# A PEER transformer's V stage: its own loading step for gates and results, four places per ring, and gathered rows handed out in other numbers

## The chip, the cores and the metric

The kernel runs on one core of a Trainium2 chip. The metric is the device time in microseconds of one execution. The kernel before took 2890.41 us (median of three runs, 2883.72 to 2892.33).

## The reference

Two layers, each with a mixer and a PEER feed-forward, over 256 latent and 256 context tokens of width 1024. The feed-forward picks 16 of 16,384 experts in each of 8 heads for every token and sums their V rows, weighted by a gate times the GELU of the product with their U rows:

```python
best_s, best_j = lax.top_k(cand_s.reshape(PEER_CHUNK, PEER_HEADS, PEER_TOPK * PEER_TOPK), PEER_TOPK)
idx = jnp.take_along_axis(cand_i.reshape(PEER_CHUNK, PEER_HEADS, PEER_TOPK * PEER_TOPK), best_j, axis=-1)
g = jax.nn.softmax(best_s, axis=-1)
a = jnp.einsum('td,thkd->thk', t, u[idx])
w = (jax.nn.gelu(a.astype(jnp.float32)) * g).astype(t.dtype)
return jnp.einsum('thk,thkd->td', w, v[idx])
```

Layer 0 has the even mixer (neighbourhood attention and a Fourier mix), layer 1 the odd mixer (differential attention). The feed-forward runs on latent and context tokens in layer 0 and on latent tokens alone in layer 1; a last norm closes the kernel.

## The kernel before

The feed-forward is done densely for most tokens. A U stage multiplies all tokens of a layer by all 16,384 rows of U; a V stage multiplies the result, weighted with gates that are zero for experts not chosen, by all rows of V. Each float32 operand is split into a high and a low part, and three products are summed.

The **U stage** (`u_prep`, `u_mm`) runs over 32 chunks of 512 experts, four loads `du` of 512 KB each, and 48 matmuls (L670 to L672) per chunk. The GELU of the result stays in SBUF for the last chunks (`dy`; 8 chunks of layer 0 and 11 of layer 1, `KEEP`) and goes to DRAM (`ad`) for the others.

The **V stage** runs over 64 chunks of 256 experts, first those whose result is resident (16 in layer 0, 22 in layer 1), then those that were written out (48 and 42). `load_v` issues on SP the loads of a chunk: the gates `dg` (384 KB in layer 0, 256 KB in layer 1), for a written-out chunk its result `dyl` (256 KB), and two halves of V, `dv`, of 512 KB each; all three rings have three places. `v_prep` makes the high part `dvh` on ACT (L724) and the low part `dvl` on DVE (L725), which frees the place in the ring `dv`. `w_prep` multiplies result and gates on DVE (L746), transposes the product on PE (L733) and splits it (`dwh`, `dwl`, and `dxh`, `dxl` for the second context tile). `v_mm` does 36 matmuls per chunk in layer 0 and 24 in layer 1, beside 6 and 4 transposes. The V pool of layer 0 takes 63 KB per partition and that of layer 1 56 KB; both lie in SBUF beside the pool of the U stage, without overlap.

The **first context tile** of layer 0 does not take part in the dense stages. Its rows are gathered, one expert per token at a time: POOL gathers `row` (512 KB, ring of four places, L549), DVE adds it up (L564 for U; `gacc`, L576, for V). A generator `rows` gives 128 rows of U for the second context tile (a gate table follows), 128 of U and 128 of V for the first. `feed(n)` asks it for n steps: 5 per U chunk for 26 chunks, 2 for the six after, 3 per V chunk, 6 in each of the eight steps of the odd mixer.

A scheduler sets the order of instructions on each engine from the program's order and from what each may start on; an engine works its own list in order. So loads of the V stage can stand among those of the U stage on SP, and rows asked for in the mixer can stand before the end of the V stage. At the end of V in layer 0, DVE adds the sums to x (`yadd` L583, L584), POOL works out the reciprocal root (L255 to L258) from `rstd` (L253), DVE normalises (`xn`, L332), and PE transposes for the odd mixer (L337).

Of the kernel before, what the change touches and what calls it, by code (L numbers as in the profile page):

```python
# [8 lines left out]
F32 = mybir.dt.float32  # L9
# [8 lines left out]
P = 128  # L18
D = 1024
# [8 lines left out]
NC = 64  # L28
# [121 lines left out]
class Builder:  # L150
# [481 lines left out]
    def dense(self, l, tables, hs, ups, yp, keep, mid, late, fin, ad, beside):  # L632

        nc, V, S, G, T = self.nc, self.V, self.S, self.G, self.T
        U = self.A[f"peer_uT{l}"]  # L640
        Vt = self.A[f"peer_v{l}"].rearrange("(c j) d -> c j d", j=P)
        nt = tables.shape[0]
        away = 2 * (NC // 2 - keep)
        cs = list(range(away, NC)) + list(range(away))
        ut, vs, ldv, gts, ys = {}, {}, {}, {}, {}
        up = ups.enter_context(self.pool("uphase", side="right"))

        def u_prep(c):
            if c >= NC // 2:
                return  # L650
            h, l_ = ut.setdefault(c, ([], []))
            for q in range(4):
                t = up.tile([P, 2, UN], F32, name="du", bufs=3)
                nc.sync.dma_start(t, U[c, :, q * 2:(q + 1) * 2])
                th = up.tile([P, 2, UN], F32R, name="duh", bufs=5)
                tl = up.tile([P, 2, UN], F32R, name="dul", bufs=5)
                S.activation(th, t, AF.Copy)  # L657
                with self.tc.high_priority():
                    V.tensor_tensor(tl, t, th.bitcast(F32), ALU.subtract)  # L659
                h += [th[:, 0, :], th[:, 1, :]]  # L660
                l_ += [tl[:, 0, :], tl[:, 1, :]]

        def u_mm(c):

            uh, ul = ut.pop(c)
            w = self.wide() if c % 2 else None
            bs = [w[:, i * 512:(i + 1) * 512] if c % 2 else self.bank("x") for i in range(2)]
            for k in range(KT):
                for (hi, lo), b in zip(hs, bs):
                    T.matmul(b, lhsT=hi[:, k, :], rhs=uh[k], start=k == 0, stop=False)  # L670
                    T.matmul(b, lhsT=hi[:, k, :], rhs=ul[k], start=False, stop=False)  # L671
                    T.matmul(b, lhsT=lo[:, k, :], rhs=uh[k], start=False, stop=k == KT - 1)  # L672
            if 2 * c < away:
                y = up.tile([P, 2, UN], F32, name="da", bufs=2)
            else:
                y = yp.tile([P, 2, UN], F32, name="dy", bufs=keep)
            if c % 2:
                S.activation(y.rearrange("p i n -> p (i n)"), w, AF.Gelu_apprx_tanh)
            else:
                for i in range(2):  # L680
                    S.activation(y[:, i, :], bs[i], AF.Gelu_apprx_tanh)
            if 2 * c < away:
                nc.sync.dma_start(ad[:, :, c * UN:(c + 1) * UN].rearrange("i p n -> p i n"), y)
            else:
                for hf in range(2):
                    ys[2 * c + hf] = y[:, :, hf * 256:(hf + 1) * 256]

        u_prep(0)
        mid()
        for c in range(NC // 2):  # L690
            u_mm(c)
            u_prep(c + 1)
            beside(c)
        ups.close()
        with self.pool("vphase") as vp:
            w = self.wide()
            pacc = [w[:, 0:512], w[:, 512:1024], self.bank("y"), self.bank("y")]
            if nt == 3:
                pacc = [self.bank("x"), self.bank("x")] + pacc[2:] + pacc[:2]

            def load_v(n):
                if n >= NC:
                    return
                c = cs[n]
                gt = vp.tile([P, nt, 256], F32, name="dg", bufs=3)
                nc.sync.dma_start(gt, tables[:, :, c * 256:(c + 1) * 256].rearrange("i p n -> p i n"))
                gts[n] = gt
                if c < away:
                    ys[c] = vp.tile([P, 2, 256], F32, name="dyl", bufs=3)
                    nc.sync.dma_start(ys[c], ad[:, :, c * 256:(c + 1) * 256].rearrange("i p n -> p i n"))  # L710
                ldv[n] = []
                for a in range(2):
                    t = vp.tile([P, D], F32, name="dv", bufs=3)
                    nc.sync.dma_start(t, Vt[2 * c + a])
                    ldv[n].append(t)

            def v_prep(n):
                if n >= NC:
                    return
                vh, vl = [], []  # L720
                for v in ldv.pop(n):
                    th = vp.tile([P, D], F32R, name="dvh", bufs=3)
                    tl = vp.tile([P, D], F32R, name="dvl", bufs=3)
                    S.activation(th, v, AF.Copy)  # L724
                    V.tensor_tensor(tl, v, th.bitcast(F32), ALU.subtract)  # L725
                    vh.append(th)
                    vl.append(tl)
                vs[n] = vh, vl

            def w_split(name, src, m):  # L730
                b = self.bank("c", m * P)
                for a in range(m):
                    T.transpose(b[:, a * P:(a + 1) * P], src(a), self.ident)  # L733
                wh = vp.tile([P, m, P], F32R, name=name + "h", bufs=2)
                wl = vp.tile([P, m, P], F32R, name=name + "l", bufs=2)
                b2 = b.rearrange("p (a t) -> p a t", a=m)
                S.activation(wh, b2, AF.Copy)
                V.tensor_tensor(wl, b2, wh.bitcast(F32), ALU.subtract)
                return wh, wl

            def w_prep(c):
                if c >= NC:
                    return
                y = ys.pop(cs[c])
                g = gts.pop(c)
                V.tensor_tensor(y, y, g[:, 0:2, :], ALU.mult)  # L746
                ws[c] = [w_split("dw", lambda a: y[:, a // 2, a % 2 * P:a % 2 * P + P], 4)]
                if nt == 3:
                    ws[c].append(w_split("dx", lambda a: g[:, 2, a * P:(a + 1) * P], 2))

            def mm(b, w, a, v, first, last):
                wh, wl = w[0][:, a, :], w[1][:, a, :]
                T.matmul(b, lhsT=wh, rhs=v[0], start=first, stop=False)  # L753
                T.matmul(b, lhsT=wh, rhs=v[1], start=False, stop=False)  # L754
                T.matmul(b, lhsT=wl, rhs=v[0], start=False, stop=last)  # L755

            def v_mm(c):
                vh, vl = vs.pop(c)
                w = ws.pop(c)

                for a, i, hf in [(a, i, hf) for a in range(2) for i in range(nt) for hf in range(2)]:
                    hs = slice(hf * 512, (hf + 1) * 512)
                    mm(pacc[2 * i + hf], w[i // 2], 2 * (i % 2) + a, (vh[a][:, hs], vl[a][:, hs]),
                       c == 0 and a == 0, c == NC - 1 and a == 1)

            ws = {}
            load_v(0)
            v_prep(0)
            load_v(1)
            w_prep(0)  # L770
            for c in range(NC):
                v_prep(c + 1)
                load_v(c + 2)
                w_prep(c + 1)
                v_mm(c)
                next(late, None)
                beside(NC // 2 + c)
            for _ in late:
                pass
            fin(pacc, vp)  # L780

    def ffn(self, l, modT, h, wp, wclose, keep, nt=2, late=iter(()), finish=None, beside=lambda c: None):
# [4 lines left out]
        with self.pool("ypool") as yp:  # L787
# [15 lines left out]

            def fin(pacc, vp):

                self.tmp = Slots((yp, "dy", keep), (vp, "dv", 3))
                g = self.gate(modT, 5, 1, "c", self.tmp, None, None)
                y = self.tmp.tile([P, D], F32, name="yadd")
                for i in range(2):
                    self.add_ffn(2 + i, pacc[2 * i:2 * i + 2], g, y)  # L810
                if finish is not None:
                    finish(pacc[4:])
# [3 lines left out]
    def run(self):  # L816
# [118 lines left out]
        def feed(n):  # L935
            for _ in range(n):
                next(rows, None)

        def beside(c):

            with tc.issue_after(routed) if c < 1 else ExitStack():
                feed(5 if c < 26 else 2 if c < NC // 2 else 3)

        def finish(pacc):
            self.norm_T(1, sc1, "x", *hl)
# [23 lines left out]
    def odd_mixer(self, cp, mp, wk, wp, sc, modT, hl, rows, feed):  # L969
# [65 lines left out]
        for c in range(4):  # L1035
            self.project_T(qT[:, c * 2:c * 2 + 2, :], self.weight2(wp, w_in[c]), hl, "x", scale=0.125)
            for m in range(2):
                rotate(qT[:, c * 2 + m, :])
            feed(6)
        for c in range(4):  # L1040
            self.project_T(kTs[1][:, c * 2:c * 2 + 2, :], self.weight2(wp, w_in[4 + c]), hl, "x")
            for m in range(2):
# [1 line left out]
            self.project(vs[1][:, :, c * 256:(c + 1) * 256], self.weight2(wp, w_in[8 + c]), hl, "x")  # L1044
            if 3 + c < 5:
                self.modulation(1, 3 + c, modT, wk, "y", 4)
            feed(6)
        feed(4 * P)

        hc = [Halves(*(rows.tile([P, KT // 2, 256], F32R, name=f"oh{c}{i}", tag="row", bufs=ROWBUFS) for i in range(2)))  # L1050
# [43 lines left out]
```

## Time and profile before

| | us |
|---|---|
| median of three runs | 2890.41 |
| the profiled execution | 2891.71 |
| its span in the trace | 2889.9 |
| layer 0, last matmul of U to last of V | 1096.7 to 1665.2 |
| layer 0, end of V to first transposes of the odd mixer | 1665.2 to 1689.1 |
| layer 1, last matmul of U to end of V | 2437.9 to about 2865 |

Over the span PE is busy for 2610.9 us (90%), DVE for 2038.6 (71%), ACT for 1310.6 (45%) and POOL for 562.0 (19%). The profile gives times in microseconds from the start of the span. SPq is the queue in which SP issues DMAs; the time of a DMA runs from its issue to its landing.

### The profile page before, as it was taken

How to read it: one execution, taken by the hardware profiler on the slowest of the kernel's cores; microseconds unless marked ns; L12 is line 12 of the kernel's file. 1: busy time of each engine (PE TensorE's matmuls, PEld its weight loads, DVE VectorE, ACT ScalarE, POOL GpSimd, SP SyncE). 2: the span in 40 equal slices, each digit the busy share in tenths (PEclk: the TensorE clock that was granted, in tenths of full speed). 3: DMA queues.
4: the chain of work that ended last, by engine and by line, in shares of the span. 5: the costliest groups of instructions: out<-in, count | busy, mean ns of one | idle time of the engine just before them, and what ended most of it. 6: DMA issues, size and time to landing. Idle time of an engine off the chain costs nothing.

```text
span 2889.9 us, 40187 instructions
## 1 busy us (share of the span) xinstructions
PE 2610.9 (90%) x14161; PEld 2134.2 (74%) x14161; DVE 2038.6 (71%) x3904; ACT 1310.6 (45%) x2226; POOL 562.0 (19%) x531
## 2 busy tenths in 40 slices
PE   6999984689999989999999969988999999998786
PEld 4776954567777767888888867868888887886665
DVE  3335699999988877887787874766998555554454
ACT  3334432358673433333333334544599743443332
POOL 0000003343433444433344430000000000000000
PEclk9999997899999999999999979999999999999999
DMA  6453466899999999999999856233778975566664
GB/s 246 132 204 86 160 243 206 278 353 345 354 374 354 358 360 351 351 351 351 338 340 358 316 184 231 91 107 127 238 223 266 313 251 180 180 205 214 201 220 140
DMA packets 354634, 735.49 MB, mean 255 GB/s; under 512 B 35312, under 2 KB 182016, under 8 KB 351872
## 3 DMA queue, kind: packets, MB, share of 16 engines
q1 hardware_dynamic: 299136, 531.56, 54.9%
q0 software_dynamic: 55296, 201.35, 19.5%
q8 instruction: 112, 1.84, 0.3%
q14 instruction: 90, 0.74, 0.1%
HBM read 664.13 MB, written 68.68 MB: 254 GB/s over the span
## 4 chain that ended last, share of the span: by engine, by line
PE 50%; issue 16%; DMA 15%; DVE 9%; POOL 6%; ACT 3%; SPq 1%; DVEq 0%; POOLq 0%; ACTq 0%
DMA dyl<-ad 7%; POOL row L549 5%; PE bank L754 4%; PE bank L755 4%; PE bank L207 4%; PE bank L206 4%; PE bank L753 4%; PE bank L208 4%; DMA du<-in_peer_uT 2%; PE bank L671 2%; PE bank L672 2%; PE wide L755 2%; PE wide L754 2%; PE wide L753 2%; PE bank L670 2%
## 5 line engine op out<-in xcount | busy, mean ns | idle before, releaser
L549 POOL DMA_INDIRECT row<-in_peer_u,gidx x256 | 346.7, 1354 | 530.2 <-DVE row L564 423.8
L724 ACT ACTIVATE dvh<-dv 128x1024 fp32r<-128x1024 f32 x256 | 269.4, 1059 | 393.6 <-DMA dv<-in_peer_v 193.6
L657 ACT ACTIVATE duh<-du 128x1024 fp32r<-128x1024 f32 x256 | 271.1, 1062 | 273.3 <-DMA du<-in_peer_uT 217.9
L659 DVE TENSOR_TENSOR dul<-du,duh 128x1024 fp32r<-128x1024 f32 x256 | 310.4, 1218 | 106.6 <-ACT duh L657 105.5
L725 DVE TENSOR_TENSOR dvl<-dv,dvh 128x1024 fp32r<-128x1024 f32 x256 | 309.2, 1222 | 93.0 <-ACT dvh L724 92.9
L564 DVE SCALAR_TENSOR_TENSOR row<-row,hc 128x1024 f32<-128x1024 f32 x256 | 307.3, 1216 | 22.0 <-DMA row<-in_peer_u,gidx 21.6
L754 PE MATMUL bank<-dvl,dwh 128*128 128x512 f32 x768 | 300.9, 392 | 0.5 <-DVE dvl L725 0.5
L755 PE MATMUL bank<-dvh,dwl 128*128 128x512 f32 x768 | 299.8, 392 | 0.0
L188 DVE TENSOR_TENSOR wl<-wt,wh 128x512 fp32r<-128x512 f32 x256 | 177.9, 700 | 157.9 <-ACT wh L187 155.5
L753 PE MATMUL bank<-dvh,dwh 128*128 128x512 f32 x768 | 265.6, 398 | 2.2 <-ACT dvh L724 1.7
L670 PE MATMUL bank<-duh,h 128*128 128x512 f32 x512 | 197.0, 411 | 65.2 <-ACT duh L657 65.1
L187 ACT ACTIVATE wh<-wt 128x512 fp32r<-128x512 f32 x256 | 160.8, 631 | 205.7 <-PE bank L207 98.9
L671 PE MATMUL bank<-dul,h 128*128 128x512 f32 x512 | 213.9, 418 | 11.9 <-DVE dul L659 11.7
L671 PE MATMUL wide<-dul,h 128*128 128x512 f32 x512 | 209.0, 408 | 10.9 <-DVE dul L659 10.9
L549 POOL DMA_INDIRECT row<-in_peer_v,gidx x128 | 170.5, 1332 | 243.7 <-DVE gacc L576 223.7
L670 PE MATMUL wide<-duh,h 128*128 128x512 f32 x512 | 207.0, 404 | 7.5 <-ACT duh L657 7.4
L206 PE MATMUL bank<-h,wh 128*128 128x256 f32 x704 | 206.0, 294 | 5.4 <-ACT hf L342 5.4
L672 PE MATMUL bank<-duh,h 128*128 128x512 f32 x512 | 208.1, 406 | 0.0
L208 PE MATMUL bank<-h,wl 128*128 128x256 f32 x704 | 204.0, 291 | 3.6 <-DVE wl L188 3.6
L207 PE MATMUL bank<-h,wh 128*128 128x256 f32 x704 | 204.5, 291 | 1.1 <-DVE h L349 1.1
L672 PE MATMUL wide<-duh,h 128*128 128x512 f32 x512 | 203.5, 397 | 0.0
L255 POOL TENSOR_TENSOR rs_t<-rstd 128x2 f32<-128x2 f32 (+1 forms) x27 | 7.4, 273 | 936.0 <-DVE rstd L253 934.7
(279 smaller groups left out, 5905.5 us busy)
## 6 DMA issues: line engine op xcount, KB each, us to landing
du<-in_peer_uT SPq DMA_DIRECT2D x256, 512.0 KB, 6.0
dv<-in_peer_v SPq DMA_DIRECT2D x256, 512.0 KB, 5.7
table<-gst SPq DMA_DIRECT2D x80, 512.0 KB, 7.0
wm<-in_w_mod SPq DMA_DIRECT2D x56, 512.0 KB, 6.9
wt<-in_peer_w_q SPq DMA_DIRECT2D x96, 256.0 KB, 3.3
dg<-table SPq DMA_DIRECT2D x64, 384.0 KB, 7.0
ad<-da SPq DMA_DIRECT2D x45, 512.0 KB, 5.4
dyl<-ad SPq DMA_DIRECT2D x90, 256.0 KB, 5.4
```

Of the source, the lines that this page charges most:

```text
L206: self.T.matmul(out, lhsT=a, rhs=b, start=k == 0 and m == 0, stop=False)
L207: self.T.matmul(out, lhsT=a, rhs=b2, start=False, stop=False)
L208: self.last = self.T.matmul(out, lhsT=a2, rhs=b, start=False, stop=k == KT - 1 and m == len(outs) - 1).ins
L549: self.G.indirect_dma_start(out=t, out_offset=None, in_=table, in_offset=bass.IndirectOffsetOnAxis(ap=idx[:, s:s + 1], axis=0))
L659: V.tensor_tensor(tl, t, th.bitcast(F32), ALU.subtract)
L670: T.matmul(b, lhsT=hi[:, k, :], rhs=uh[k], start=k == 0, stop=False)
L671: T.matmul(b, lhsT=hi[:, k, :], rhs=ul[k], start=False, stop=False)
L672: T.matmul(b, lhsT=lo[:, k, :], rhs=uh[k], start=False, stop=k == KT - 1)
L725: V.tensor_tensor(tl, v, th.bitcast(F32), ALU.subtract)
L753: T.matmul(b, lhsT=wh, rhs=v[0], start=first, stop=False)
L754: T.matmul(b, lhsT=wh, rhs=v[1], start=False, stop=False)
L755: T.matmul(b, lhsT=wl, rhs=v[0], start=False, stop=last)
```

## The change

`load_v` keeps the two halves of V. A new `load_g` takes over gates and results, and runs one chunk further ahead (`c + 3` where V has `c + 2`). The rings `dg`, `dyl` and `dv` have four places. Ahead of the loop stand the V loads of two chunks and the gates and results of three. Rows of the first context tile are asked for 2 and 3 in turn per V chunk (160 over the stage in place of 192), and 8 and 12 per step of the odd mixer (80 in place of 48).

```diff
+            def load_g(n):
+                if n >= NC:
+                    return
+                c = cs[n]
+                gts[n] = vp.tile([P, nt, 256], F32, name="dg", bufs=4)
+                nc.sync.dma_start(gts[n], tables[:, :, c * 256:(c + 1) * 256].rearrange("i p n -> p i n"))
+                if c < away:
+                    ys[c] = vp.tile([P, 2, 256], F32, name="dyl", bufs=4)
+                    nc.sync.dma_start(ys[c], ad[:, :, c * 256:(c + 1) * 256].rearrange("i p n -> p i n"))
+
             def load_v(n):
                 if n >= NC:
                     return
-                c = cs[n]
-                gt = vp.tile([P, nt, 256], F32, name="dg", bufs=3)
-                nc.sync.dma_start(gt, tables[:, :, c * 256:(c + 1) * 256].rearrange("i p n -> p i n"))
-                gts[n] = gt
-                if c < away:
-                    ys[c] = vp.tile([P, 2, 256], F32, name="dyl", bufs=3)
-                    nc.sync.dma_start(ys[c], ad[:, :, c * 256:(c + 1) * 256].rearrange("i p n -> p i n"))
                 ldv[n] = []
                 for a in range(2):
-                    t = vp.tile([P, D], F32, name="dv", bufs=3)
-                    nc.sync.dma_start(t, Vt[2 * c + a])
+                    t = vp.tile([P, D], F32, name="dv", bufs=4)
+                    nc.sync.dma_start(t, Vt[2 * cs[n] + a])
                     ldv[n].append(t)
...
             load_v(0)
+            load_g(0)
+            load_g(1)
+            load_v(1)
+            load_g(2)
             v_prep(0)
-            load_v(1)
             w_prep(0)
             for c in range(NC):
                 v_prep(c + 1)
                 load_v(c + 2)
+                load_g(c + 3)
                 w_prep(c + 1)
...
-                self.tmp = Slots((yp, "dy", keep), (vp, "dv", 3))
+                self.tmp = Slots((yp, "dy", keep), (vp, "dv", 4))
...
-                feed(5 if c < 26 else 2 if c < NC // 2 else 3)
+                feed(5 if c < 26 else 2 if c < NC // 2 else 2 + c % 2)
...
-            feed(6)
+            feed(8)
...
-            feed(6)
+            feed(12)
```

The fourth places make the V pool larger: 72 KB per partition in layer 0 and 64 KB in layer 1. As built, it then reaches into the addresses of the U pool in both layers (in layer 0 it ends at 174,432 where the U pool starts at 167,904; in layer 1 at 149,344 where the U pool starts at 147,424). Before, it ended at 165,216 and 141,152, below the same starts.

On SP, at the hand-over from U to V in layer 0, this stands before (`du` is a load of U; `dg`, `dv` and `dyl` are the V stage's):

```order
L654 DMA du_8854<-in_peer_uT0 128x1024
L706 DMA dg_9823<-table0_4361 128x3x256
L714 DMA dv_9825<-in_peer_v0 128x1024
L714 DMA dv_9827<-in_peer_v0 128x1024
L654 DMA du_8860<-in_peer_uT0 128x1024
L706 DMA dg_9837<-table0_4361 128x3x256
L714 DMA dv_9839<-in_peer_v0 128x1024
L706 DMA dg_9868<-table0_4361 128x3x256
L710 DMA dyl_10961<-ad0_4362 128x2x256
L710 DMA dyl_11039<-ad0_4362 128x2x256
L654 DMA du_9399<-in_peer_uT0 128x1024
```

The same place on SP of the changed kernel:

```order
L654 DMA du_9727<-in_peer_uT0 128x1024
L654 DMA du_9733<-in_peer_uT0 128x1024
L654 DMA du_9739<-in_peer_uT0 128x1024
L654 DMA du_9745<-in_peer_uT0 128x1024
L717 DMA dv_9823<-in_peer_v0 128x1024
L717 DMA dv_9825<-in_peer_v0 128x1024
L706 DMA dg_9827<-table0_4361 128x3x256
L706 DMA dg_9829<-table0_4361 128x3x256
L717 DMA dv_9831<-in_peer_v0 128x1024
L717 DMA dv_9833<-in_peer_v0 128x1024
L706 DMA dg_9835<-table0_4361 128x3x256
```

The first V load has moved from ahead of the last 21 `du` to behind the last one, where it waits for the last matmul of the U stage, since its place lies in the U pool's addresses; in layer 1 it is the same (`dv_22431` stands behind the last `du`). On PE, 36 matmuls of V stand ahead of the last matmul of U in layer 0 before and none in the changed kernel.

In the V stage of layer 1, among written-out chunks, SP has this before (numbers tell the tiles apart; those of a chunk and the next differ by 50):

```order
L714 DMA dv_24833<-in_peer_v1 128x1024
L710 DMA dyl_24931<-ad1_17939 128x2x256
L714 DMA dv_24835<-in_peer_v1 128x1024
L706 DMA dg_25079<-table1_17938 128x2x256
L714 DMA dv_24883<-in_peer_v1 128x1024
L710 DMA dyl_24981<-ad1_17939 128x2x256
```

On DVE at the same place before (L746 is the product of result and gates, written into `dyl`):

```order
L746 TENSOR_TENSOR dyl_24881<-dyl_24881,dg_24879 128x512
L725 TENSOR_TENSOR dvl_24776<-dv_24735,dvh_24775 128x1024
L725 TENSOR_TENSOR dvl_24822<-dv_24783,dvh_24821 128x1024
L738 TENSOR_TENSOR dwl_24844<-bank_24838,dwh_24843 128x512
L746 TENSOR_TENSOR dyl_24931<-dyl_24931,dg_24929 128x512
L725 TENSOR_TENSOR dvl_24826<-dv_24785,dvh_24825 128x1024
```

SP of the changed kernel:

```order
L717 DMA dv_24835<-in_peer_v1 128x1024
L709 DMA dyl_24939<-ad1_17939 128x2x256
L717 DMA dv_24883<-in_peer_v1 128x1024
L706 DMA dg_25137<-table1_17938 128x2x256
L717 DMA dv_24885<-in_peer_v1 128x1024
L709 DMA dyl_24989<-ad1_17939 128x2x256
```

DVE of the changed kernel:

```order
L749 TENSOR_TENSOR dyl_24889<-dyl_24889,dg_24887 128x512
L728 TENSOR_TENSOR dvl_24780<-dv_24735,dvh_24779 128x1024
L728 TENSOR_TENSOR dvl_24826<-dv_24783,dvh_24825 128x1024
L741 TENSOR_TENSOR dwl_24848<-bank_24842,dwh_24847 128x512
L749 TENSOR_TENSOR dyl_24939<-dyl_24939,dg_24937 128x512
L728 TENSOR_TENSOR dvl_24830<-dv_24785,dvh_24829 128x1024
```

A `dyl` load stood behind the first half of a V pair and stands now behind the second half of the pair before; the product stays directly ahead of the low part of a second half (`dv_24785`), one chunk older in relation to its `dyl`.

At the end of V in layer 0, DVE has this before, from the last `yctx` to the norm:

```order
L583 TENSOR_TENSOR yctx_14906<-wide_9818,gate_9930 128x512 x2
L576 SCALAR_TENSOR_TENSOR gacc_12894<-row_16183,ijgc_73,gacc_12894 128x1024
L253 TENSOR_SCALAR rstd_14841<-ss_14837 128x2
L584 TENSOR_TENSOR xl1_9945<-xl1_9945,yctx_14906 128x512 x2
L576 SCALAR_TENSOR_TENSOR gacc_12894<-row_16186,ijgc_73,gacc_12894 128x1024
L576 SCALAR_TENSOR_TENSOR gacc_12894<-row_16189,ijgc_73,gacc_12894 128x1024
L332 TENSOR_SCALAR xn_14835<-xl2_9947,rstd_14841 128x1024
L332 TENSOR_SCALAR xn_14836<-xl3_9949,rstd_14841 128x1024
```

DVE of the changed kernel, from the same `yctx`:

```order
L583 TENSOR_TENSOR yctx_14810<-wide_9818,gate_9932 128x512 x2
L576 SCALAR_TENSOR_TENSOR gacc_13381<-row_16165,ijgc_73,gacc_13381 128x1024
L253 TENSOR_SCALAR rstd_14745<-ss_14741 128x2
L584 TENSOR_TENSOR xl1_9947<-xl1_9947,yctx_14810 128x512 x2
L576 SCALAR_TENSOR_TENSOR gacc_13381<-row_16168,ijgc_73,gacc_13381 128x1024
L576 SCALAR_TENSOR_TENSOR gacc_13381<-row_16171,ijgc_73,gacc_13381 128x1024
L576 SCALAR_TENSOR_TENSOR gacc_13381<-row_16174,ijgc_73,gacc_13381 128x1024
L576 SCALAR_TENSOR_TENSOR gacc_13381<-row_16177,ijgc_73,gacc_13381 128x1024
L576 SCALAR_TENSOR_TENSOR gacc_13381<-row_16180,ijgc_73,gacc_13381 128x1024
L576 SCALAR_TENSOR_TENSOR gacc_13381<-row_16183,ijgc_73,gacc_13381 128x1024
L332 TENSOR_SCALAR xn_14739<-xl2_9949,rstd_14745 128x1024
L332 TENSOR_SCALAR xn_14740<-xl3_9951,rstd_14745 128x1024
```

Between `rstd` and `xn` stand six additions of rows where two stood. Counted from the last `dvl` of the stage, `xn` stands behind the 20th row and not the 15th, and the first `yadd` behind the eighth and not the seventh. On POOL the gathers of four of the rows (`row_16180` to `row_16189`) stand now between the steps of the reciprocal root (L255 to L258), where all but one stood ahead of them.

## Rows read from the trace of the kernel before

**Rows 1.** The page's chain that ended last, by line.

```profile
DMA dyl<-ad 7%; POOL row L549 5%; PE bank L754 4%; PE bank L755 4%; PE bank L207 4%; PE bank L206 4%; PE bank L753 4%; PE bank L208 4%; DMA du<-in_peer_uT 2%; PE bank L671 2%; PE bank L672 2%; PE wide L755 2%; PE wide L754 2%; PE wide L753 2%; PE bank L670 2%
```

**Rows 2.** Stretches: length; PE, PEld, DVE, ACT, POOL busy (count); PE clock, DMA share, GB/s.

```profile
1005.00:1097.00 92.00, 79.11 (x327) 59.34 (x325) 69.99 (x96) 31.71 (x36) 47.23 (x32) 0.98 0.95 351
1160.00:1590.00 430.00, 429.72 (x2034) 355.60 (x2034) 346.23 (x414) 139.56 (x196) 176.63 (x132) 1.00 0.97 348
2460.00:2560.00 100.00, 100.00 (x474) 82.67 (x474) 51.40 (x51) 43.70 (x50) 0.00 (x0) 1.00 0.57 178
2600.00:2840.00 240.00, 201.47 (x907) 156.02 (x907) 115.49 (x130) 83.55 (x97) 0.00 (x0) 1.00 0.67 212
```

**Rows 3.** SP's timeline (start, us) at 998, then DMA issues of 990 to 1025.

```profile
998.28 0.38 SPq L706 DMA_DIRECT2D dg<-table  x1
...
dv<-in_peer_v SPq DMA_DIRECT2D x6, 512.0 KB, 9.0
dg<-table SPq DMA_DIRECT2D x5, 384.0 KB, 14.8
dyl<-ad SPq DMA_DIRECT2D x3, 256.0 KB, 9.6
```

**Rows 4.** PE's timeline, last matmuls of U and V, layer 0; a stretch after 3 us' idling.

```profile
1096.73 0.40 PE L672 MATMUL wide<-duh,h 128*128 128x512 f32 x1
...
1665.20 0.39 PE L755 MATMUL wide<-dvh,dxl 128*128 128x512 f32 x1
...
1056.00:1060.00 4.00, 3.79 (x10) 3.03 (x11) 4.00 (x7) 0.27 (x1) 2.26 (x2) 0.60 0.70 226
```

**Rows 5.** PE's timeline at layer 1's hand-over, landing of `dv` 2445 to 2560, two costs.

```profile
2437.93 0.39 PE L672 MATMUL wide<-duh,h 128*128 128x512 f32 x1
2438.16 1.04 PE L733 MATMUL bank<-c_ident,dy 128*128 128x128 f32 x8
2439.92 0.50 PE L753 MATMUL wide<-dvh,dwh 128*128 128x512 f32 x1 [0.73 <-ACT dwh L737]
...
DMA to landing us min/median/max: 3.4/3.5/4.0
...
L746 DVE TENSOR_TENSOR dy<-dy,dg x4: 683/685/694, 2427.8 to 2440.8; 128x512 f32<-128x512 f32 x4
...
L724 ACT ACTIVATE dvh<-dv 128x1024 fp32r<-128x1024 f32 x256 | 269.4, 1059 | 393.6 <-DMA dv<-in_peer_v 193.6
```

**Rows 6.** DVE's and POOL's timelines at layer 0's end; PE's wait there (us, times, longest).

```profile
1654.33 1.30 DVE L725 TENSOR_TENSOR dvl<-dv,dvh 128x1024 fp32r<-128x1024 f32 x1 [0.23 <-ACT dvh L724]
1668.66 0.68 DVE L583 TENSOR_TENSOR yadd<-bank,gate 128x512 f32<-128x512 f32 x1
1681.83 0.16 DVE L253 TENSOR_SCALAR rstd<-ss 128x2 int32<-128x2 int32 x1
1688.27 1.42 DVE L332 TENSOR_SCALAR xn<-xl,rstd 128x1024 f32<-128x1024 f32 x2 [2.57 <-POOL rstd L258]
...
1673.20 1.14 POOL L549 DMA_INDIRECT row<-in_peer_v,gidx  x1 [1.46 <-DVE gacc L576]
1675.59 0.94 POOL L549 DMA_INDIRECT row<-in_peer_v,gidx  x1 [1.25 <-DVE gacc L576]
...
PE bank L337 <- DVE xn L332: 22.7, 1, 22.7
```

**Rows 7.** Chain of waits at 2705, `dyl` loads of 2570 to 2850, PE's wait there.

```profile
2705.45 4.35 DMA dyl<-ad
...
2710.50 1.23 DVE dvl L725
...
L710 SPq DMA_DIRECT2D dyl<-ad x38: 377/386/426, 2571.4 to 2845.6; - x38
...
DMA to landing us min/median/max: 4.2/5.0/7.0
...
PE wide L754 <- DVE dvl L725: 41.5, 36, 3.2
```

## The prediction, made before the changed kernel ran

> **What bounds the kernel now.** I read the chain of waits first. Its largest line is a load, `dyl`, with 7% of the span, ahead of the gathers of the first context tile [rows 1]; every other line is PE work. Then I cut the span into stretches to see who is full where [rows 2]. At the end of layer 0's U stage PE works 79.11 of 92 us while the DMA engines are busy for 0.95 of it at 351 GB/s: transfers bound it. In its V stage PE works 429.72 of 430 us, so PE is the bound, though the DMA share is 0.97. One chunk there is 42 PE instructions (36 matmuls and 6 transposes): 430 / 2034 x 42 = 8.88 us. In layer 1's V stage there are two halves. With resident results PE works all of 100 us at a DMA share of 0.57, and a chunk of 28 instructions takes 100 / 474 x 28 = 5.91 us. With results that come back from DRAM it works 201.47 of 240.
>
> The cause of that last gap is in [rows 7]: a `dyl` load takes 4.35 us, the product on DVE follows, then a `dvl` of 1.23 us, which frees a place for a `dv` load, behind which SP issues the next `dyl`. The loads go out every (2845.6 - 2571.4) / 37 = 7.41 us, and PE waits 36 times for `dvl`, 41.5 us in all. So 7.41 - 5.91 = 1.50 us per chunk is lost to one loop through SP, DMA and DVE, over 38 loads.
>
> **Part 1: hand-over from U to V, layer 0.** Before, V loads start on SP at 998.28, long ahead of the last U matmul at 1096.73 [rows 3, 4]. Five `dg`, six `dv` and three `dyl` go out by 1025 [rows 3], 5 x 384 + 6 x 512 + 3 x 256 KB = 5.9 MB (decimal). At 351 GB/s [rows 2] that is up to 17 us; I take 15, since the last of them share their time with what follows. In the changed kernel all V loads wait for the last U matmul, because the larger V pool lies over the U pool. U then loses about 15 us, of which 36 V matmuls were PE work to be done anyway, and ends near 1083 (PE's idle time in that stretch, 12.9 us, and those matmuls, 36/42 x 8.88 = 7.6 us, allow it). Then PE waits for the first `dv` and `dg`: in [rows 3] these landed in 9.0 and 14.8 us, with U loads beside them, and in the quieter layer 1 `dv` lands in 3.5 [rows 5]. I take a landing of 7 us in between, then high part 1.06 [rows 5], low part 1.23 [rows 7] and 1.5 for product and transposes: a gap of 11 us. Behind a gap PE runs at the lower of its two clock levels: after an idle time of 3 us at 1053 a stretch of 4 us had a granted clock of 0.60 and ten matmuls [rows 4], where 4 us at 0.23 us each [rows 5] hold 17. The seven lost are 1.6 us; after a longer gap I take 2.5. The first chunks fill their rings from nothing, and I add 3 us of waits. With 64 chunks at 8.88 us (568.3) V ends at 1083 + 11 + 2.5 + 3 + 568.3 = 1667.8; before it ended at 1665.6 [rows 4]. **+2 us**. If loads land in 3.5 us and U gains the whole 17, it is -6; if U is held by something else and ends at 1090 with slower first chunks, +12.
>
> **Part 2: fewer rows per V chunk.** The 32 rows (512 KB each) taken out of the V stage relieve DMA and DVE, but PE is busy there for 429.72 of 430 us: **0 us** there. They come later.
>
> **Part 3: end of V, layer 0, to the odd mixer.** PE's last V matmul starts at 1665.20 and PE then waits 22.7 us for `xn` [rows 4, 6]. DVE's last `dvl` is at 1654.33, the first `yadd` at 1668.66, `rstd` at 1681.83, `xn` at 1688.27 [rows 6]. With the fourth place of `dv` the last `dvl` still waits for PE through the three places of `dvl`, so it stays as far ahead of the end of V. In that stretch a gather goes out every 1675.59 - 1673.20 = 2.39 us, when an addition on DVE has freed a place [rows 6]. The order puts `xn` behind the 20th and not the 15th row: five rows more at 2.0 to 2.4 us, **+10 us**. One of the five is ahead of `yadd`; the others stand between `rstd` and `xn`, with gathers among the steps of the reciprocal root, so they are waited for in turn. If DVE catches up beforehand, since it had seven rows fewer to do in the stage, it is +4; if each interleaved gather takes its own time to land, +13. The 80 rows asked for in the mixer cost it nothing more: the order has them all out by the first `h1`.
>
> **Part 4: hand-over, layer 1.** Before, PE goes from its last U matmul (2437.93) through the transposes (2438.16) to the first V matmul (2439.92) [rows 5]: 1.76 us, 0.73 of it idle. Now the first loads go out after 2438.2: two `dv` and then `dg`. With the third load on SP after 1.0 us and some 1.25 MB ahead of or beside it (3.5 us at 351 GB/s, and a share of the 3.5 us that a lone `dv` takes), I take a landing at 6.0 us, product 0.69 [rows 5], and 1.76 from the first transpose to the first matmul: 8.4 us, or 6.7 more than now. The gap costs clock again, 2.5 as in part 1. Then eight chunks take in all gates and products that stood in the U stage before: 25 gates of 256 KB and 16 halves of V of 512 KB are 15.2 MB in 8 x 5.91 = 47 us, 322 GB/s against 351 that were seen [rows 2]. That nearly fits, and I add 2 us. **+11 us**, from +7 (no crowding, quick landing) to +18 (each first chunk waits for its gates).
>
> **Part 5: the `dyl` loop, layer 1.** A fourth place looks as if it gave the load more time. The order says otherwise: `dyl` now stands behind a `dv` that takes the place of four halves earlier and not three, and its product stands ahead of a `dvl` one chunk older. Before: `dvl` of `dv_24735`, load `dv_24833`, `dyl_24931`, its product, `dvl` of `dv_24785`. After: `dvl` of `dv_24735`, load `dv_24835`, `dyl_24939`, its product, `dvl` of `dv_24785`. From one `dvl` to the next there is one load, one product and one `dvl` in both, and the same other loads beside it. So the period stays 7.41 us, with one cycle fewer, as the lead grew by a chunk: **-1.5 us** (-5 to +2).
>
> The Trainium skill (Perfetto Trace Analysis, Optimization Strategy) says that a gap that repeats on the engine that should be full can mean too few buffers for the next tile. The repeating gap is there (1.50 us), and by that rule a fourth place would remove it; the sum would then be rival A's. The order of the two queues is why I don't follow it.
>
> **Sum.** 2 + 0 + 10 + 11 - 1.5 = +21.5. Against the profiled execution's 2891.7 that is 2913.2; the median of the runs is 1.3 lower, so **2912 us**.
>
> **Rivals.** *A, the loop breaks (faster).* If a `dyl` is there before DVE asks for it, the period of 7.41 falls to PE's 5.91: 38 x 1.50 = 57 us. The other parts cost 2 + 10 + 11 = 23, so 2891.7 + 23 - 57 = 2858, or 2856 by the median. For it speaks that gates and results have a step of their own with a chunk's more lead; against it, that SP issues in order and the `dv` ahead of each `dyl` waits for the same `dvl`. It decides sooner, too: each 0.1 us off a landing of 5.0 is worth 3.8 us, so a landing of 4.4 pays for the rest, and below about 3.5 PE becomes the bound.
>
> *B, the hand-overs are cheap (no difference).* The pools overlap, but U in layer 0 ends 17 us sooner and the first loads land in the 3.5 us of an idle queue: -6 there, +7 in layer 1, +4 at the end of V, -1.5 in the loop: +3.5, 2894 by the median. For it: queues stand empty at both places. Against it: gathers go on in layer 0, and the first landings there took 9 to 15 us.
>
> *C, layer 0 gets nothing back (slower still).* If U's end is held by ACT, DVE or the gathers and not by the V loads, U ends at 1090, and the gap is not paid for: 7 us more, 2919 by the median.
>
> By the Trainium skill (the same page and section) regimes with different bounds can gain from interleaving, which this change undoes. Layer 1's rows agree (0.57 of DMA in V); in layer 0 both stages stand at 0.95 or more, and I let the row decide. By the rule alone the 36 matmuls, 7.6 us, would be lost there as well, some 2919.
>
> **Chances.** The forecast 0.58, A 0.14, B 0.16, C 0.12. About 0.3% (8.7 us) is what a measurement of this kernel can tell from no change, so 'same' is 2882 to 2899. A is faster, B the same, the forecast and C slower: 0.14, 0.16, 0.70. The range leaves out A and a little above C: 2887 to 2930.
>
> **What would show it.** Right: the first V matmul 8 to 11 us after the last of U in both layers, with a granted clock near 0.6 behind it; PE's wait for `xn` near 33 us; `dyl` loads of layer 1 still about 7.4 us apart and PE's wait for `dvl` near 41 us. Wrong: a period near 6 us (A); a gap under 4 us, or the last U matmul of layer 0 well before 1080 (B); the last U matmul of layer 0 at 1088 or later (C). What would upset the sum most is a different landing time of `dyl`, since 38 loads carry it.

## The result and the profile after

The changed kernel took **2902.9 us** (median of five runs, 2901.89 to 2909.36) against 2890.41: a ratio of **1.0057, 95% interval 1.0042 to 1.0072**, so slower by 0.6%, some 16 us by the ratio. The profiled execution has a span of 2900.1 us where 2889.9 stood.

Cut at PE's first and last matmuls of each stage, the two spans divide so (us; stage times, here and below, are differences of times rounded to 0.1 us, so their last digit can be off by one):

| stage | before | after | difference |
|---|---|---|---|
| start to first U matmul, layer 0 | 524.9 | 517.6 | -7.3 |
| U, layer 0 | 571.8 | 561.8 | -10.0 |
| last U matmul to last V matmul, layer 0 | 568.5 | 584.6 | +16.1 |
| last V matmul to the odd mixer's transposes | 23.9 | 33.3 | +9.4 |
| odd mixer, to first U matmul of layer 1 | 329.6 | 331.9 | +2.3 |
| U, layer 1 | 419.2 | 419.5 | +0.3 |
| last U matmul to first V matmul, layer 1 | 2.0 | 9.7 | +7.7 |
| V, layer 1 | 431.6 | 423.4 | -8.2 |
| last V matmul to the end | 18.4 | 18.3 | -0.1 |

At the hand-over of layer 0, where the answer to [rows 4] stands, PE's timeline of the changed kernel is this (start, us, engine, line, what; the idle time before it in brackets, with what ended it):

```profile
1079.39 0.40 PE L672 MATMUL wide<-duh,h 128*128 128x512 f32 x1
1094.21 1.12 PE L736 MATMUL bank<-c_ident,dy 128*128 128x128 f32 x4 [14.42 <-DVE dy L749]
1095.12 0.63 PE L736 MATMUL bank<-c_ident,dg 128*128 128x128 f32 x2
1096.01 0.80 PE L756 MATMUL bank<-dvh,dwh 128*128 128x512 f32 x1 [0.26 <-ACT dwh L740]
```

PE stands still for 14.42 us, until the first gates have come and been multiplied. SP's timeline, the product on DVE, what the first V load waits for (SP's own waits of 1000 to 1180) and the stretch in which the gates are on their way:

```profile
1079.82 0.80 SPq L717 DMA_DIRECT2D dv<-in_peer_v  x2
1080.67 1.07 SPq L706 DMA_DIRECT2D dg<-table  x2
1081.78 2.70 SPq L717 DMA_DIRECT2D dv<-in_peer_v  x2
1084.52 5.54 SPq L706 DMA_DIRECT2D dg<-table  x2
1090.11 4.77 SPq L926 DMA_DIRECT2D xl<-xd  x4
...
1093.46 0.69 DVE L749 TENSOR_TENSOR dy<-dy,dg 128x512 f32<-128x512 f32 x1 [2.61 <-DMA dg<-table]
...
SPq L717 <- PE wide L672: 4.8, 1, 4.8
...
1082.00:1094.00 12.00, 0.00 (x0) 0.00 (x0) 4.14 (x6) 2.11 (x2) 2.81 (x3) 0.59 1.02 390
```

The first V load waits for the last matmul of U (L672). From the issue of the first gates to the product that waits for them it is 12.8 us. The DMA issues between 1079 and 1100 (count, KB, median us to landing; the 14.5 is that of the later gates), against [rows 3]:

```profile
dv<-in_peer_v SPq DMA_DIRECT2D x5, 512.0 KB, 12.1
xl<-xd SPq DMA_DIRECT2D x4, 512.0 KB, 12.7
dg<-table SPq DMA_DIRECT2D x4, 384.0 KB, 14.5
...
row<-in_peer_u,gidx POOLq DMA_INDIRECT x6, 8.8
```

All that a ring can take goes out at once, with the gathers and, from 1090 on, four loads of x beside it. The DMA engines are not quiet at all. What follows is good: PE's stretches of the V stage (columns as in [rows 2]) are full from there on, and the main stretch is as before.

```profile
1079.00:1096.00 17.00, 2.33 (x10) 1.45 (x8) 7.65 (x12) 3.77 (x5) 4.83 (x5) 0.65 1.01 375
...
1097.00:1160.00 63.00, 62.52 (x302) 51.78 (x301) 48.03 (x72) 23.29 (x35) 16.62 (x14) 0.99 0.99 365
1160.00:1590.00 430.00, 430.00 (x2041) 358.31 (x2040) 343.52 (x414) 140.31 (x196) 157.47 (x126) 1.00 0.96 343
```

At the end of V in layer 0, the answer to [rows 6] on DVE, then POOL, then the wait of PE (total, times, longest):

```profile
1681.91 0.17 DVE L253 TENSOR_SCALAR rstd<-ss 128x2 int32<-128x2 int32 x1
1681.98 1.29 DVE L584 TENSOR_TENSOR xl<-xl,yctx 128x512 f32<-128x512 f32 x2
1683.18 4.00 DVE L576 SCALAR_TENSOR_TENSOR gacc<-row,ijgc,gacc 128x1024 f32<-128x1024 f32 x3
1688.29 1.28 DVE L576 SCALAR_TENSOR_TENSOR gacc<-row,ijgc,gacc 128x1024 f32<-128x1024 f32 x1 [1.10 <-DMA row<-in_peer_v,gidx]
1692.63 1.28 DVE L576 SCALAR_TENSOR_TENSOR gacc<-row,ijgc,gacc 128x1024 f32<-128x1024 f32 x1 [3.06 <-DMA row<-in_peer_v,gidx]
1695.15 1.28 DVE L576 SCALAR_TENSOR_TENSOR gacc<-row,ijgc,gacc 128x1024 f32<-128x1024 f32 x1 [1.24 <-DMA row<-in_peer_v,gidx]
1696.51 1.42 DVE L332 TENSOR_SCALAR xn<-xl,rstd 128x1024 f32<-128x1024 f32 x2
```

```profile
1689.70 0.19 POOL L258 TENSOR_TENSOR rstd<-rs_t,rstd 128x2 f32<-128x2 f32 x1
1690.40 0.97 POOL L549 DMA_INDIRECT row<-in_peer_v,gidx  x1 [0.50 <-issue]
1691.40 0.20 POOL L255 TENSOR_TENSOR rs_t<-rstd 128x2 f32<-128x2 f32 x1
...
1695.74 0.74 POOL L258 TENSOR_TENSOR rstd<-rs_t,rstd 128x2 f32<-128x2 f32 x1
...
PE bank L337 <- DVE xn L332: 32.1, 1, 32.1
```

`rstd` on DVE is hardly later than before (16.6 us behind the last V matmul before, 17.9 here); the six additions behind it take until 1696.4, three of them waiting for a row to land, and gathers now go out between the steps of the root. The last step of the root, on POOL, ends at 1696.48 as well, where before it ended at 1688.24, with the norm waiting for it [rows 6]. So additions and root are late together; which of them would delay the norm alone was not shown.

At the hand-over of layer 1, the answer to [rows 5], and the clock behind it:

```profile
2448.66 0.40 PE L672 MATMUL wide<-duh,h 128*128 128x512 f32 x1
2455.92 1.11 PE L736 MATMUL bank<-c_ident,dy 128*128 128x128 f32 x4 [6.87 <-DVE dy L749]
...
2458.43 0.78 PE L756 MATMUL wide<-dvh,dwh 128*128 128x512 f32 x1
```

```profile
2458.00:2462.00 4.00, 4.00 (x13) 3.23 (x12) 3.42 (x5) 1.22 (x2) 0.00 (x0) 0.50 1.09 375
2462.00:2466.00 4.00, 4.00 (x17) 3.24 (x15) 1.35 (x2) 1.06 (x1) 0.00 (x0) 0.85 1.06 376
```

What the first V load waits for is in SP's own waits of 2440 to 2875:

```profile
SPq L717 <- PE wide L672: 11.6, 1, 11.6
```

That is the last matmul of U (L672). Behind the gap, thirty matmuls run in eight us, where 0.23 us each would give 35: the lower clock cost 1.2 us.

In the second half of layer 1's V stage, the answers to [rows 2, 7] are the stretch, the `dyl` loads from 2560 on, their landing, and the waits of 2585 to 2870, with one line of the same waits before:

```profile
2600.00:2840.00 240.00, 208.18 (x943) 162.23 (x943) 117.70 (x132) 87.63 (x101) 0.00 (x0) 1.00 0.67 217
...
L709 SPq DMA_DIRECT2D dyl<-ad x38: 377/386/436, 2585.4 to 2849.2; - x38
...
DMA to landing us min/median/max: 3.4/4.8/5.5
```

```profile
ACT dvh L727 <- PE bank L758: 173.8, 79, 3.6
DVE dyl L749 <- DMA dyl<-ad: 132.0, 38, 4.3
...
PE wide L757 <- DVE dvl L728: 32.7, 32, 1.6
```

```profile
ACT dvh L724 <- DMA dv<-in_peer_v: 174.2, 72, 6.4
```

The loads come every (2849.2 - 2585.4) / 37 = 7.13 us. The loop is still there: DVE waits for every one of the 38 `dyl` loads. ACT now waits for PE to free a place of `dvh`, where before it had waited 174.2 us for `dv` to land: the fourth place did make V's halves come in time, and PE gained little from it.

### The profile page after: what moved, and what is told of

It is laid out like the page before. It is cut to its first block, busy times and chain, and to the rows that moved or that the text cites. A ratio compares the mean times of both kernels' runs of the same rounds, so it can differ in the third digit from the quotient of the medians.

```text
span 2900.1 us, 40158 instructions
## 1 busy us (share of the span) xinstructions
PE 2610.7 (90%) x14161; PEld 2141.5 (74%) x14161; DVE 2040.2 (70%) x3904; ACT 1310.5 (45%) x2226; POOL 544.8 (19%) x531
## 4 chain that ended last, share of the span: by engine, by line
PE 49%; issue 16%; DMA 14%; DVE 10%; POOL 5%; ACT 4%; SPq 1%; DVEq 0%; POOLq 0%; ACTq 0%
DMA dyl<-ad 6%; POOL row L549 5%; PE bank L206 3%; PE bank L207 3%; PE bank L208 3%; PE bank L756 3%; PE bank L757 3%; PE bank L758 3%; PE bank L628 3%; PE bank L671 2%; PE bank L672 2%; PE wide L671 2%; PE wide L672 2%; PE wide L670 2%; PE bank L670 2%
## 5 line engine op out<-in xcount | busy, mean ns | idle before, releaser
L756 PE MATMUL bank<-dvh,dwh 128*128 128x512 f32 x768 | 298.4, 399 | 0.7 <-ACT dvh L727 0.5
L671 PE MATMUL wide<-dul,h 128*128 128x512 f32 x512 | 209.9, 410 | 11.3 <-DVE dul L659 11.3
L672 PE MATMUL bank<-duh,h 128*128 128x512 f32 x512 | 208.8, 408 | 0.0
L672 PE MATMUL wide<-duh,h 128*128 128x512 f32 x512 | 204.9, 400 | 0.0
L549 POOL DMA_INDIRECT row<-in_peer_v,gidx x128 | 155.9, 1218 | 252.6 <-DVE gacc L576 227.0
L628 PEld LDWEIGHTS bank<-goj,goi 128*128 128x128 f32 x1280 | 163.4, 192 | 26.0 <-ACT gst L629 14.0
```

What stands on the lines that cost most here:

```text
L549: self.G.indirect_dma_start(out=t, out_offset=None, in_=table, in_offset=bass.IndirectOffsetOnAxis(ap=idx[:, s:s + 1], axis=0))
```

## The experiments

**Which part of the change does it.** First each part alone. The loading part:

```diff
-                feed(5 if c < 26 else 2 if c < NC // 2 else 2 + c % 2)
+                feed(5 if c < 26 else 2 if c < NC // 2 else 3)
...
-            feed(8)
+            feed(6)
...
-            feed(12)
+            feed(6)
```

> The changed kernel with the old numbers of rows (3 per V chunk, 6 per step of the mixer), so the loading part alone. Theory P (the pools' overlap does it): every engine's order is that of the changed kernel but for tile numbers, so 2902 to 2907 us, V to the odd mixer of layer 0 33 us, hand-over gaps 16 and 10 us. Rival R (the rows' new numbers delay the norm at the end of V): about 2893 us, with V to the mixer back at 24 us. If the 7 us by which the first U matmul came earlier in the changed kernel belong to the program, it is at 517 to 518 us again; if they are chance, it may lie anywhere from 517 to 525.

Measured: 2906.88 us against 2883.76 on the same chip, ratio 1.0076 (1.0052 to 1.0100); 33.7 us from V to the mixer, gaps of 14.3 and 9.5 us. The first U matmul is at 522.2. And the part with the rows, the same edit the other way round on the kernel before:

> The kernel before with the new numbers of rows (2 and 3 in turn, 8 and 12), so that part alone. Theory P: the order of every engine is that of before, so no difference (2882 to 2893 us), V to the odd mixer 24 us. Rival R: about 9 us slower, 2900 us, with V to the mixer at 33 us. First U matmul: at 525 us if its time belongs to the program, anywhere from 517 to 525 if it is chance.

Measured: 2884.58 us against 2883.76, ratio 0.9999 (0.9982 to 1.0016); V to the mixer 23.1 us, first U matmul at 523.2. The order of instructions of this kernel and of the one before is the same on all five engines, tile numbers aside. So rival R falls: the numbers of rows asked for per step move nothing. The two pairs with equal orders also show what one profile can tell: 517.6 and 522.2 us to the first U matmul with the changed loading, 524.9 and 523.2 without. Over all eleven profiles here it is 517.6 to 525.7 us, with and without the changed loading. The -7.3 of the table is for the most part chance.

**The overlap of the pools.** The changed kernel with rings cut to fit below the U pool:

```diff
-                gts[n] = vp.tile([P, nt, 256], F32, name="dg", bufs=4)
+                gts[n] = vp.tile([P, nt, 256], F32, name="dg", bufs=3)
...
-                    t = vp.tile([P, D], F32, name="dv", bufs=4)
+                    t = vp.tile([P, D], F32, name="dv", bufs=3 if nt == 3 else 4)
...
-                self.tmp = Slots((yp, "dy", keep), (vp, "dv", 4))
+                self.tmp = Slots((yp, "dy", keep), (vp, "dv", 3 if nt == 3 else 4))
```

> The changed kernel with rings cut so that the V pool ends below the U pool: layer 0 has dg 3, dyl 4, dv 3, layer 1 has dg 3, dyl 4, dv 4. V loads stand again among the last U loads on SP. Theory P: the gaps of 16 and 10 us between U and V are gone (under 3 us), V to the mixer of layer 0 is 24 to 27 us, the period of the dyl loads in layer 1 stays 7.1 to 7.4 us: 2880 to 2893 us. Rival S (load_g as a step of its own, with its other order on SP, is what costs): 2898 us or more, though the gaps are gone.

Measured: 2886.91 us, ratio 1.0015 (0.9998 to 1.0031). Fifteen V loads stand again ahead of the last `du` of layer 0. V's first matmul comes 2.0 us after U's last in layer 1, V to the mixer takes 25.5 us, `dyl` loads come every 7.12 us. Rival S falls: `load_g` costs nothing that can be measured. The reverse is the kernel before with one place more for `dv`:

```diff
-                    t = vp.tile([P, D], F32, name="dv", bufs=3)
+                    t = vp.tile([P, D], F32, name="dv", bufs=4)
...
-                self.tmp = Slots((yp, "dy", keep), (vp, "dv", 3))
+                self.tmp = Slots((yp, "dy", keep), (vp, "dv", 4))
```

> The kernel before with a fourth place for dv alone: its V pool overlaps the U pool in layer 0 and not in layer 1. Theory P: layer 0 shows the changed kernel's gap (last U matmul about 15 us earlier, first V matmul 10 to 17 us behind it, V to the mixer 31 to 33 us), layer 1 is as before (hand-over 2 us): some 6 us from the hand-over and 8 from the end of V, 2898 to 2905 us. Rival D (the fourth place of dv pays in layer 1's loop): dyl period under 6.5 us, 2870 us or less.

Measured: 2905.16 us, ratio 1.0081 (1.0051 to 1.0110). Layer 0 has the gap (first V matmul 11.5 us after the last of U) and 32.7 us from V to the mixer; layer 1 hands over in 2.0 us. `dyl` comes every 7.24 us: rival D falls too. The sizes do not fit as well as the sign. This kernel's profiled execution (2896.7 us) is the fastest of its four runs, the other three took 2904.5 to 2911.0, and the medians differ by 21 us although the gap of layer 1 is not there: no trace shows where those runs lose the rest. In the changed kernel's case as well, the runs differ by more than the profiles.

PE's wait at the end of V in this kernel and, without overlap, in the one with cut rings:

```profile
PE bank L337 <- DVE xn L332: 31.5, 1, 31.5
```

```profile
PE bank L337 <- DVE xn L332: 24.5, 1, 24.5
```

**The rows ahead of the norm.** Is it rows that PE waits for there? The changed kernel with the last rows held on DVE behind the norm:

```diff
-            V.tensor_scalar(xn[i], self.x[2 * s + i], r[:, i:i + 1], None, op0=ALU.mult)
+            self.normed = V.tensor_scalar(xn[i], self.x[2 * s + i], r[:, i:i + 1], None, op0=ALU.mult).ins
...
+        def held(n):
+            with tc.issue_after(normed):
+                feed(n)
...
-                feed(5 if c < 26 else 2 if c < NC // 2 else 2 + c % 2)
+                feed(5 if c < 26 else 2 if c < NC // 2 else 3 + c % 2)
...
-            self.odd_mixer(cp, mp, wk, self.w1, sc1, mod1, hl, l0, feed)
+            normed = self.normed
+            self.odd_mixer(cp, mp, wk, self.w1, sc1, mod1, hl, l0, held)
...
-            feed(8)
+            feed(3)
...
-            feed(12)
+            feed(3)
```

> The changed kernel with the rows asked for in the mixer (18) held behind the norm, the product not held. If the 33 us from V to the mixer come from rows that stand ahead of the norm (20 by the order, 5 here), it falls to 15 to 18 us, and the time to 2884 to 2893 us. If they come from the overlap of the pools or the fourth place of dv in another way, it stays at 28 us or more, and the time above 2898 us.

Measured: 2899.16 us, ratio 1.0047 (1.0033 to 1.0061). V to the mixer falls from 33.3 to 13.0 us, so the rows, by their additions on DVE and their gathers on POOL, are shown to be what PE waits for. But the mixer grows from 331.9 to 346.1 us, most of the gain is given back, and the 2884 to 2893 us expected were missed.

**The loop of `dyl`.** The kernel before, rings of three, with the product held back on DVE:

```diff
-                    V.tensor_tensor(tl, v, th.bitcast(F32), ALU.subtract)
+                    low[n] = V.tensor_tensor(tl, v, th.bitcast(F32), ALU.subtract).ins
...
-                V.tensor_tensor(y, y, g[:, 0:2, :], ALU.mult)
+                with self.tc.issue_after(low[c - 1]) if c else ExitStack():
+                    V.tensor_tensor(y, y, g[:, 0:2, :], ALU.mult)
...
-            ws = {}
+            ws, low = {}, {}
```

> The kernel before, with the product of result and gates of chunk n held on DVE behind the last dvl of chunk n-1 (before, it stood three chunks ahead). Rings stay at three places. Theory P (the loop from dvl over the dv load, the dyl load and the product back to dvl sets 7.1 to 7.4 us, whatever the number of places): the loop is cut, dyl loads come every 5.9 to 6.0 us, PE's wait for dvl in layer 1 (34 to 41 us) falls under 5 us, V of layer 1 takes 380 to 390 us in place of 427 to 432: 2838 to 2850 us. Rival D (the landing of dv and dyl as such is too slow for 5.9 us, three places are too few): period still 6.8 us or more, 2870 to 2890 us.

Measured: **2844.73 us** against 2885.86 on the same chip, ratio 0.9863 (0.9833 to 0.9892): faster than both kernels. V of layer 1 takes 380.9 us, and its 39 `dyl` loads come every (2797.7 - 2571.1) / 38 = 5.96 us on the mean. PE works every microsecond of the second half at a DMA share of 0.80, and its wait for `dvl` is no longer among the waits:

```profile
2600.00:2780.00 180.00, 180.00 (x847) 146.75 (x846) 112.06 (x121) 79.95 (x91) 0.00 (x0) 1.00 0.80 266
...
ACT dvh L724 <- PE bank L756: 104.9, 62, 1.8
DVE dvl L725 <- ACT dvh L724: 88.6, 82, 1.5
...
DMA to landing us min/median/max: 4.1/4.3/6.0
```

A `dyl` load still needs 4.3 us to land, nearly as long as before; nobody waits for it any more. Rival D falls. The hold does one thing more: of layer 1's gate loads 5 and not 21 stand ahead of the last `du`; what that does alone was not tried. The same hold on the changed kernel:

> The changed kernel with the same hold of the product. Theory P: the loop goes here too (period 5.9 to 6.0), V of layer 1 380 to 395 us with its crowded start, while the gap at both hand-overs and the 33 us from V to the mixer stay: 2855 to 2870 us, so 12 to 22 us above the kernel before with that hold. Rival D: with four places the transfers are early enough and this one is the faster of the two.

Measured: 2862.32 us, ratio 0.9922 (0.9892 to 0.9953). V of layer 1 takes 381.9 us; the gaps (16.6 and 9.6 us) and V to the mixer (32.4 us) stay. With the loop gone from both, the change costs 20.6 us by the spans (2860.6 against 2840.0), 5.9 of them ahead of the first U matmul (525.7 against 519.8), and 17.6 us by the medians. And the loading step with rings that fit, the hold and the old numbers of rows, all three edits from above:

> All that can be kept of the change without the overlap, with the product held: load_g as its own step, rings that end below the U pool (layer 0 dg 3, dyl 4, dv 3; layer 1 dg 3, dyl 4, dv 4), rows as before. Theory P: hand-overs without gaps (2 us in layer 1), V to the mixer 24 to 26 us, V of layer 1 about 380 us, so the same as the kernel before with the hold alone: 2838 to 2850 us, and the change's loading step is worth nothing once the loop is cut. Rival D (the longer lead is worth something once the loop is cut): 2835 us or less.

Measured: 2846.48 us, ratio 0.9865 (0.9842 to 0.9889), as with the hold alone. A step of its own for gates and results is worth nothing here. Last, the hold of the product and the hold of the rows (18 of them) on the kernel before:

> The kernel before with the held product, and with the rows that the mixer asks for (18, as V asks for 3 and 4 in turn) held on DVE behind the norm at the end of V in layer 0; the mixer asks for 3 per step. If the rows ahead of the norm are what PE waits for there, V to the mixer falls from 24 to 14 to 17 us and the 18 additions (1.28 us each) find room in the mixer, which stays at 330 us or grows by up to 10: 2828 to 2845 us. If the norm waits for the sums and the reciprocal root alone, V to the mixer stays over 20 us and nothing is won.

Measured: 2851.19 us, ratio 0.9884 (0.9850 to 0.9918). That is above the 2828 to 2845 us expected, and no faster than the hold of the product alone. V to the mixer takes 13.1 us in place of 25.0, but the mixer 345.8 in place of 330.5. Two lines suggest where the gain went: the waits of 1675 to 1790 have one at the weights' loads of 29.1 us, against 8.6 of before in 1688 to 1790, and PE is idle while the DMA engines are full:

```profile
ACT wh L187 <- DMA wt<-in_odd_w_in: 29.1, 14, 6.5
```

```profile
1702.00:1720.00 18.00, 11.62 (x70) 9.73 (x68) 13.67 (x24) 5.13 (x9) 9.01 (x9) 0.91 0.95 362
```

It looks as if the mixer's first weights had been loaded in the time that PE stood waiting for the norm. Moving those loads was not tried.

## Why the prediction was right, and where its steps were off

It forecast 2912 us, slower; 2902.9 was measured. The direction and the three places named were right, and the sum was too high.

**Part 1, hand-over in layer 0: right in its sum, its pieces off.** U shrank by 10.0 us where 14 was worked out from its end, the gap was 16.6 where 11 was, and the waits of 3 us behind it did not come. The sign named, 8 to 11 us in both layers, held in layer 1 alone. The landing was mis-sized: 7 us were assumed, and from the first gates' issue to their product it was 12.8. They stand behind two halves of V on SP, and with a share of 1.02 the DMA engines were full: four halves, four gates and the four gathers issued from 1078 to 1085 are 5.8 MB, some 15 us at the 390 GB/s of that stretch (an estimate). With a fourth place for `dv` alone the first gates stand ahead of the halves; there they landed in 7.2 us, and the gap was 11.5. From the first U matmul to the last V matmul, 568.5 + 571.8 = 1140.3 before and 1146.4 after; the equal-order pair has 1145.1 and 1142.3. Over all eleven profiles it is 1140.3 to 1145.1 in the six with V loads ahead of the end of U, and 1141.6 to 1146.4 in the five without. So the hand-over of layer 0 costs about nothing: what V no longer takes from U's transfers, U gives back. By the Trainium skill (Perfetto Trace Analysis, Optimization Strategy) performance may gain from interleaving regimes with different busiest engines, so a loss could be expected here too; the 1145.1 and 1142.3 show none, and one shows in layer 1 (2.0 and 9.7 us).

**Part 2, fewer rows per chunk: right number, wrong step.** The text said that rows are taken out of V and come later. None moved.

**Part 3, end of V: right.** +10 was forecast, +9.4 measured, and rows ahead of the norm, with gathers among the steps of the root, were the mechanism, as the hold showed. The text left open why the order had five rows more there. The runs narrow it down: it is not the new numbers (23.1 us with them alone) but the larger V pool in layer 0 (32.7 us with a fourth place of `dv` alone, 25.5 with rings that fit). In every kernel here the fourth place of `dv` in layer 0 goes with the overlap, and it also gives the code that adds the sums a fourth temporary place. Which of these puts more rows at the end of V, and how the scheduler comes to it, was not shown.

**Part 4, hand-over in layer 1: the gap right, what follows mis-sized.** 6.7 us more were forecast and 7.7 measured, with gates landing in 5.0 to 7.6 us where 6.0 was assumed. Clock and crowding were put at 4.5 us. The clock cost 1.2. With the loop cut, V took 381.9 us from its first matmul in the changed kernel and 380.9 in the one before, so both together cost about 1 us, and the crowded chunks nearly nothing (their loads come to 14.9 MB, not 15.2), although the DMA share was 1.03 from 2458 to 2480.

**Part 5, the loop: the mechanism right, its size off.** The period stayed above 7 us with three places (7.41 and 7.25) and four (7.13, 7.14, 7.12), and fell to PE's pace as soon as the product was held, with three places. PE's wait for `dvl` fell from 41.5 to 32.7 us, where one cycle less (1.5 us) was forecast. Part of that is chance: the equal-order kernel had 34.4 without any fourth place. Against that one the difference is 1.7 us. The trace of before was a slow specimen of this stage, with one interval of 9.38 us, and the forecast took its mean for the kernel's.

**The sum.** The profiled pair differs by 10.2 us, 11.3 less than forecast. Less than forecast: 7.3 ahead of the first U matmul (chance, for the most part), 2.5 in part 4 (the gap 1.0 longer, the rest 3.5 shorter) and 7.7 in the loop (V of layer 1 is 8.2 shorter in spite of 1.0 at its start, where 1.5 was forecast). More than forecast: 4.1 in part 1 (chance too, by the eleven profiles), and 2.0 in the mixer, part 3 and U of layer 1. The timed runs differ by more than the profiles: the two kernels with this order have ratios of 1.0057 and 1.0076, 16 and 22 us.

**Rival A** fell by the runs with a fourth place and without the hold: none came near 6 us. By the Trainium skill's rule on repeating gaps (same section) too few buffers can be the reason; here the repeating gap had another cause, an order of two queues, and the measurement decides. **Rival B** had layer 1's hand-over about right (+7; 7.7 and about 1 were measured). In layer 0 U did end 17.3 us sooner, 7.3 of them ahead of the first U matmul, but the gap was 16.6 us and not under 4, so its -6 did not come; nor did its +4 at the end of V. **Rival C** was wrong: the last U matmul came at 1079.4.

## What to carry to other kernels

A larger ring is not free even where SBUF has room at that moment: where it reached into the addresses of the stage before, every early load of the next stage was lost. In layer 1 that cost 7.7 us; in layer 0 the earlier stage gave the time back, and what cost there was that more gathered rows stood ahead of the norm at the end of V. Before adding a place to a ring, follow the loop through the queues. Here a load stood in order behind another, whose place was freed by an instruction that itself stood behind the first load's consumer; it ran at 7.1 to 7.4 us per cycle with three places or four, and holding the consumer back (a few lines, 1.4%) did what the fourth place did not. And compare at least two profiles of the same order before a stage's time is taken for the kernel's.

## What the runs showed that was not expected

Asking for 80 gathers in the mixer in place of 48, and for 160 in V in place of 192, changed no engine's order. The first gates into empty rings, in a queue that was thought quiet, were 12.8 us on their way (`dg`, 384 KB, at a DMA share of 1.02); in layer 1's steady stage a `dg` of 256 KB landed in 2.7. After 6.87 idle microseconds and eight transposes PE's granted clock was 0.50 for four microseconds and 0.85 for the next four, a loss of 1.2 us.
